# A hybrid attention and pooling layer in f32r parts: column sums and the bias look-up as two-part products, a norm's sums seven K steps later, one place for the indexer's query weights

## The chip, the core and the metric

One core of one Trainium2 chip runs the whole layer as one program. The metric is the device time of one execution in microseconds (us); a kernel's time is the median of its runs. A difference under 0.2% (2.0 us here) is about what a measurement of this kernel can't tell from no change.

## What is computed

A decoder layer on 272 tokens (16 meta tokens and 256 of the sequence) of width 2048, in float32:

```
p = h @ W_in        # q | latent c_kv (256) | indexer queries (16 x 64) | indexer key | head weights | pool channels
c_kv = rms_norm(c_kv, g)                      # sum of squares over the 256 latent channels
score = sum_h w[t,h] * relu(q_idx . k_idx);   keep the top 64 keys of each query
logits = q_abs . c_kv * s + rel_bias[t5_bucket(t - s)];   softmax;   values
mix = concat(attention, pooled windows) @ W_o
h = layer_norm(alpha*h + mix)                 # mean and variance over 2048 channels
f = conv_gated_ffn(h)                         # up product, width 3 conv, gelu gate, down product
out = layer_norm(alpha*h + f)
```

## The kernel before

Every product is made of parts in f32r: a value is split into an upper part (a copy in f32r, made on ACT, called hi or `[:, 0]`) and a remainder (value less upper part, made on DVE, lo or `[:, 1]`). A K step of a product is three matmuls: hi with hi, and the two mixed ones. `product` (lines 305 to 315) does this for 16 K steps in an order given by a list of places (`K_PROJ`, `K_O`, `K_UP`). A tile's flag `turned` sets which of the two mixed matmuls comes first.

A stream of weight blocks of 1 MB feeds it: SP issues the load of a raw block (3 buffers), ACT writes the upper parts (line 190) and DVE the remainders (line 191), in two halves of 1024 columns, into one of 3 split tiles. `weights()` hands out a block and starts the one two ahead. Where in a split tile the two parts start is given in bytes by `place`; `places` picks it for each block. The first 8 blocks are the indexer's queries and have eight places in `QUERIES`, of which the first is `(88, False)`.

The tokens are the partitions' free axis: activations lie as channels by tokens, so a sum over channels is a matmul with a matrix of ones (`sum_rows`, line 357). These matmuls, the one of the bias look-up (line 456) and the one of line 795 are in plain float32, and not in parts.

- Queries, lines 486 to 510: for each of 8 blocks j, the product in three pieces (9, 3 and 4 K steps) with the two heads of block j - 1 between them (`dots`, line 469: matmuls, two relus on ACT into a tile `rl`, two updates of `score` on DVE). After j = 0 comes `latent_scale` (line 427: the two squares `sqs` are summed, a DVE transposition into `r`, line 430 on DVE, and a power on POOL, line 431); after j = 1 come `latent_norm` and `relative_bias` (line 450: two small loads, the look-up as matmul of the table with a one-hot matrix, a strip to DRAM and back as `bias`).
- The tiles made by `temp` (`wt`, `sq`, `r`, `rb`, `rl`, `rb_sb`, `oh`, `strip` and later ones) share four buffers under one tag, "t", given out in the order of the program.
- Output and first norm, lines 740 to 800: 16 output blocks m; after m = 3 POOL adds four of them, after m = 4 their column sum gives an offset `acc` (lines 795 and 796). `about_k(m)` then takes the offset off (DVE, line 768), squares (ACT, 770), adds to the running sums `s1` and `s2` on POOL (774, 776) and makes a tile `fold` of the channel in two parts (ACT 781, DVE 782). The last channel, m = 15, is not added on POOL: its value and its square go as own matmuls into the sums.
- Up product, lines 968 to 1009: the first 8 up blocks (f < 4, two halves each) multiply `folded`, so that the norm's scale and shift can be put on behind the product (`unfold`). In the first of them, after 5 K steps, comes `deviation` (line 804): four float32 matmuls, two transpositions, some small DVE steps, a power on POOL (813), two row spreads (370). The second half of the third up block's remainder waits for it (`later`, line 223). Then `normalise` (825 to 830) makes the normed channels `h_parts`, some behind each block, for the up blocks from f = 4 on.

Each engine runs its queue in the order that a planner fixed when the program was built: it goes by the order of the program and by its own estimates of when an instruction can start, and an instruction whose inputs are late holds up those behind it on its engine.

Of the kernel before, what the change touches and what calls it, by code (L numbers as in the profile page):

```python
# [25 lines left out]
H = 8  # L26
# [87 lines left out]
def places(n, kind):  # L114
# [5 lines left out]
    if n < 8:  # L120
        return place(*QUERIES[n])
# [5 lines left out]
QUERIES = ((88, False), (96, True), (72, True), (152, True), (216, True), (40, False), (168, False), (232, True))  # L127
# [6 lines left out]
def tile_layer(ctx, tc, xt, w_first, w_proj, w_uk, w_uv, w_pool, w_o, w_up, w_down, cols, rows, rel_bias, onehot, out):  # L134
# [214 lines left out]
    ones = sb.tile([P, P], F32, name="ones")  # L349
    nc.vector.memset(ones, 1.0)  # L350
# [6 lines left out]
    def sum_rows(s):  # L357

        ps = small()
        for n, t in enumerate(s):  # L360
            nc.tensor.matmul(ps[:, :t.shape[1]], ones, t, start=n == 0, stop=n == len(s) - 1)
        return ps[:, :W]
# [48 lines left out]
    for j in range(2):  # L411
# [5 lines left out]
        sqs.append(sq)  # L417
    widx = ap_.tile([P, 2, HI], F32, name="widx")
# [8 lines left out]
    def latent_scale():  # L427
        r = temp([P, W], "r")
        to_partitions(r, sum_rows(sqs))
        nc.vector.tensor_scalar(v, r[:, ::32], 1.0 / C, EPS, op0=ALU.mult, op1=ALU.add)  # L430
        nc.gpsimd.tensor_tensor(v, v, half, op=ALU.pow)
# [18 lines left out]
    def relative_bias():  # L450
        rb_sb = temp([32, H], "rb_sb")
        nc.sync.dma_start(rb_sb, rel_bias)
        oh = temp([32, T], "oh")
        nc.sync.dma_start(oh, onehot)
        ps = small()
        nc.tensor.matmul(ps[:H, :T], rb_sb, oh, start=True, stop=True)
# [29 lines left out]
    for j in range(8):  # L486
# [17 lines left out]
        if j == 0:  # L504
            latent_scale()
        if j == 1:
            latent_norm()
            relative_bias()
# [250 lines left out]
    nc.gpsimd.memset(sums[:, 2 * NQ:], 0.0)  # L759
# [5 lines left out]
    def about_k(m):  # L765
# [7 lines left out]
        elif 1 < m < KT - 1:  # L773
            nc.gpsimd.tensor_tensor(s1, s1, yd, op=ALU.add)
        if 0 < m < KT - 1:
# [9 lines left out]
        return yd, sq  # L785

    for m in range(1, KT):
        output(m)
        if m == KC - 1:
            nc.gpsimd.tensor_tensor(acc, y[:, 0, Q0:], y[:, 1, Q0:], op=ALU.add)  # L790
            for k in range(2, KC):
                nc.gpsimd.tensor_tensor(acc, acc, y[:, k, Q0:], op=ALU.add)
        if m == KC:
            ps = small()
            nc.tensor.matmul(ps[:, :NQ], ones, acc, start=True, stop=True)
            nc.scalar.activation(acc, ps[:, :NQ], AF.Copy, scale=1.0 / (KC * P))
        if m >= KC:
            while len(folded) < min(m + 1, 2 * (m - KC + 1)):
                last_two = about_k(len(folded))

# [3 lines left out]
    def deviation():  # L804
        mean, square = (of_token[:, j * NQ:j * NQ + W] for j in range(2))
        for j, r in enumerate((mean, square)):
            to_partitions(r, sum_rows([sums[:, j * NQ:j * NQ + W], last_two[j]]))
# [135 lines left out]
    for item in plan:  # L943
# [48 lines left out]
        if f < FOLDED:  # L992
            k = 0
            if f + half_ == 0:
                product(ps[:, :NE], hl, folded, 0, NE, K_UP, k1=5)
                deviation()
                k = 5
# [110 lines left out]
    for i in range(2):  # L1108
# [25 lines left out]
        if i:  # L1134

            shift = small()
            nc.tensor.matmul(shift, ones[:1, :], gb[7][:1, :], start=True, stop=False)
# [71 lines left out]
```

## Time and profile before

| | |
|---|---|
| time, median of 3 runs | 1020.82 us (1019.65 to 1021.59) |
| the profiled execution: its time, its span | 1020.17 us, 1018.4 us |
| PE, matmul busy | 1010.6 us, 99% |
| DVE, ACT, POOL busy | 889.6 us (87%), 622.0 us (61%), 187.8 us (18%) |
| chain that ended last, by engine | PE 95%, issue 2%, DMA 1%, POOL 1% |
| HBM | 232.50 MB read, 230 GB/s over the span |

The span is the time from the first to the last instruction of the profiled execution; its time is 1.8 us longer. Starts in a timeline are us from the span's start. A matmul's duration in a row includes the pipeline behind it, so the cost of one is read from start to start: a K step (called a triple below) runs from one L312 row to the next.

### The profile page before, as it was taken

To read this page: it belongs to the slowest core of one execution; us is meant where nothing else is said; L and a number is where in the kernel's file an instruction comes from. 1 tells how busy PE (TensorE), PEld (TensorE's weight loads), DVE (VectorE), ACT (ScalarE), POOL (GpSimd) and SP (SyncE) were. 2 spreads that over 40 slices of the span, in tenths; PEclk is the share of its full clock that TensorE was granted. 3 is DMA by queue.
4 is the path that set the end of the run, shared out by engine and by line. 5 is a ranking of instruction groups with operands and counts; after the bars stand their busy time and mean duration, and the time that the engine had idled before them with its cause. 6 is when DMAs were issued, how large, how long until landed. Compare 5 with 4: busy or idle time off the path is not lost.

```text
span 1018.4 us, 19198 instructions
## 1 busy us (share of the span) xinstructions
PE 1010.6 (99%) x7644; PEld 963.1 (95%) x7644; DVE 889.6 (87%) x1401; ACT 622.0 (61%) x1000; POOL 187.8 (18%) x245
## 2 busy tenths in 40 slices
PE   9999999999999999999999999999999999999997
PEld 8999999999999999999999999999999999999986
DVE  6878668758879998999999998999999998999876
ACT  6656346655549765655666656666566666666675
POOL 1200014125430022111121111211112111120031
PEclk9999999999999999999999999999999999999998
DMA  8755643454654668989888798887988779888774
GB/s 327 253 190 213 226 159 108 135 203 166 207 177 155 207 192 256 291 288 291 288 295 279 275 301 271 284 288 274 302 278 288 275 283 287 279 288 283 285 223 160
DMA packets 59755, 250.28 MB, mean 246 GB/s; under 512 B 21735, under 2 KB 22417, under 8 KB 32657
## 3 DMA queue, kind: packets, MB, share of 16 engines
q1 hardware_dynamic: 34592, 230.42, 63.1%
q0 software_dynamic: 7888, 16.14, 8.3%
q10 hardware_dynamic: 17184, 2.49, 1.5%
q8 instruction: 60, 0.98, 0.4%
q14 instruction: 31, 0.25, 0.1%
HBM read 232.50 MB, written 2.11 MB: 230 GB/s over the span
## 4 chain that ended last, share of the span: by engine, by line
PE 95%; issue 2%; DMA 1%; POOL 1%; ACT 0%; DVE 0%; SPq 0%; POOLq 0%; ACTq 0%
PE mm L315 47%; PE mm L312 24%; PE at L909 6%; PE at L910 6%; PE at L911 6%; DMA wraw<-in_w_proj 1%; PE mm L962 1%; PE mm L961 1%; PE mm L963 1%; DMA wraw<-in_w_first 1%; POOL gb L1028 0%; PE mm L614 0%; PE at L649 0%; PE at L475 0%; PE at L476 0%
## 5 line engine op out<-in xcount | busy, mean ns | idle before, releaser
L191 DVE TENSOR_TENSOR whl<-wraw,whl 128x1024 fp32r<-128x1024 f32 (+1 forms) x415 | 484.8, 1204 | 40.0 <-ACT whl L190 39.3
L190 ACT ACTIVATE whl<-wraw 128x1024 fp32r<-128x1024 f32 (+1 forms) x415 | 401.4, 1014 | 117.6 <-DMA wraw<-in_w_up 26.0
L315 PE MATMUL mm<-hp,whl 128*128 128x258 f32 x2560 | 448.8, 279 | 0.0
L315 PEld LDWEIGHTS mm<-hp,whl 128*128 128x128 f32 x2560 | 389.7, 188 | 2.9
L312 PE MATMUL mm<-hp,whl 128*128 128x258 f32 x1280 | 356.5, 279 | 0.0
L312 PEld LDWEIGHTS mm<-hp,whl 128*128 128x128 f32 x1280 | 240.3, 188 | 2.8
L315 PE MATMUL mm<-xp,whl 128*128 128x256 f32 (+5 forms) x768 | 139.6, 282 | 0.3 <-DVE whl L191 0.3
L315 PEld LDWEIGHTS mm<-xp,whl 128*128 128x128 f32 x768 | 118.3, 188 | 0.9 <-DVE whl L191 0.5
L312 PE MATMUL mm<-xp,whl 128*128 128x256 f32 (+5 forms) x384 | 111.3, 290 | 0.0
L881 POOL TENSOR_TENSOR forms<-za 128x128 f32<-128x128 f32 x20 | 21.8, 1091 | 298.1 <-DVE za L862 231.9
L312 PEld LDWEIGHTS mm<-xp,whl 128*128 128x128 f32 x384 | 72.3, 188 | 1.0 <-issue 0.5
L910 PE MATMUL at<-whl,gp 128*128 128x512 f32 x180 | 70.5, 392 | 0.0
L911 PE MATMUL at<-whl,gp 128*128 128x512 f32 x180 | 70.4, 392 | 0.0
L844 ACT ACTIVATE z<-mm,cv 128x256 f32<-128x256 f32 x40 | 22.5, 563 | 77.8 <-PE mm L315 76.9
L909 PE MATMUL at<-whl,gp 128*128 128x512 f32 x180 | 69.1, 394 | 0.0
L844 ACT ACTIVATE za<-mm,cv 128x256 f32<-128x256 f32 x40 | 22.6, 564 | 65.6 <-PE mm L315 57.2
L884 POOL TENSOR_TENSOR forms<-za 128x128 f32<-128x128 f32 x20 | 20.4, 1018 | 196.7 <-DVE za L862 196.7
L315 PE MATMUL mm<-mixp,whl 128*128 128x258 f32 x256 | 45.4, 279 | 0.0
L315 PE MATMUL mm<-fold,whl 128*128 128x260 f32 x256 | 45.3, 279 | 0.0
L315 PE MATMUL mm<-mixa,whl 128*128 128x258 f32 x256 | 45.2, 278 | 0.0
L911 PEld LDWEIGHTS at<-whl,gp 128*128 128x128 f32 x180 | 33.8, 188 | 8.0
L910 PEld LDWEIGHTS at<-whl,gp 128*128 128x128 f32 x180 | 33.7, 187 | 6.4
(341 smaller groups left out, 1607.2 us busy)
## 6 DMA issues: line engine op xcount, KB each, us to landing
wraw<-in_w_up SPq DMA_DIRECT2D x88, 1024.0 KB, 5.1
wraw<-in_w_down SPq DMA_DIRECT2D x80, 1024.0 KB, 6.5
wraw<-in_w_proj SPq DMA_DIRECT2D x24, 1024.0 KB, 5.1
wraw<-in_w_o SPq DMA_DIRECT2D x16, 1024.0 KB, 4.9
y<-v POOLq DMA_DIRECT2D x27, 256.0 KB, 8.3
y<-u POOLq DMA_DIRECT2D x18, 256.0 KB, 4.8
wraw<-in_w_first SPq DMA_DIRECT2D x8, 304.0 KB, 5.5
x<-in_xt SPq DMA_DIRECT2D x1, 2176.0 KB, 8.2
```

The source lines that it names most:

```text
L190: upper = nc.scalar.activation(hl[:, 0, c], like(raw[:, c], hl, c), AF.Copy)
L191: lower = nc.vector.tensor_tensor(hl[:, 1, c], like(raw[:, c], hl, c), hl[:, 0, c].bitcast(F32), op=ALU.subtract)
L312: nc.tensor.matmul(ps, wh, ah, start=n == 0, stop=False)
L315: nc.tensor.matmul(ps, a, b, start=False, stop=i == 1 and n == KT - 1)
L844: nc.scalar.activation(z, src[:, 2:NQ], AF.Identity, bias=col(C_B, j), scale=col(C_W, 3 * j + 2))
L881: nc.gpsimd.tensor_tensor(s[:, 0], a21, a22, op=ALU.add)
L884: nc.gpsimd.tensor_tensor(s[:, 3], a11, a21, op=ALU.subtract)
L909: nc.tensor.matmul(ps, a[:, 0, i], hl[:, 0, w], start=j == 0, stop=False)
L910: nc.tensor.matmul(ps, a[:, 0, i], hl[:, 1, w], start=False, stop=False)
L911: nc.tensor.matmul(ps, a[:, 1, i], hl[:, 0, w], start=False, stop=j == n - 1)
L961: nc.tensor.matmul(downs[i], a[:, 0, r], hl[:, 0, w], start=k == 0, stop=False)
L962: nc.tensor.matmul(downs[i], a[:, 0, r], hl[:, 1, w], start=False, stop=False)
```

## The change

- The eight query blocks all lie at `place(88)`, not turned; `QUERIES` goes.
- `sum_rows` takes an upper part and a remainder, and makes two f32r matmuls with f32r ones instead of as many float32 ones as there were tiles.
- The two squares of the latent are added on POOL and split (ACT, POOL) before their sum. `latent_scale` and the look-up come after block j = 1, `latent_norm` after j = 2; the two small loads come after j = 0, and the one-hot matrix is loaded twice, into 64 partitions.
- The look-up multiplies the table's two parts, stacked in 64 partitions, by an f32r copy of the one-hot matrix (copied on POOL).
- The offset's sum is split (ACT, DVE) before its product.
- `about_k(15)` adds to `s1` and `s2` on POOL as the others do; both sums are then split (one ACT copy, one DVE subtraction of 2 x 258 columns), and `deviation` comes after 12 K steps of the first up block instead of 5.

```diff
@@ -118,13 +118,12 @@
     if n < 8:
-        return place(*QUERIES[n])
+        return place(88)
-QUERIES = ((88, False), (96, True), (72, True), (152, True), (216, True), (40, False), (168, False), (232, True))
@@ -346,20 +345,20 @@
-    ones = sb.tile([P, P], F32, name="ones")
-    nc.vector.memset(ones, 1.0)
+    ones = sb.tile([P, P], F32R, name="ones")
+    nc.vector.memset(ones.bitcast(F32), 1.0)
-    def sum_rows(s):
+    def sum_rows(hi, lo):
-        ps = small()
-        for n, t in enumerate(s):
-            nc.tensor.matmul(ps[:, :t.shape[1]], ones, t, start=n == 0, stop=n == len(s) - 1)
-        return ps[:, :W]
+        ps, one = small(), ones
+        nc.tensor.matmul(ps[:, :hi.shape[1]], one, hi, start=True, stop=False)
+        nc.tensor.matmul(ps[:, :lo.shape[1]], one, lo, start=False, stop=True)
+        return ps[:, :hi.shape[1]]
@@ -415,6 +414,10 @@
+    sq_parts = [ap_.tile([P, W], F32R, tag="t", name="sqp", bufs=4, padded_shape=[P, KW]) for _ in range(2)]
+    nc.gpsimd.tensor_tensor(sqs[0], sqs[0], sqs[1], op=ALU.add)
+    nc.scalar.activation(sq_parts[0], sqs[0], AF.Copy)
+    nc.gpsimd.tensor_tensor(sq_parts[1], sqs[0], sq_parts[0].bitcast(F32), op=ALU.subtract)
@@ -426,7 +429,7 @@
-        to_partitions(r, sum_rows(sqs))
+        to_partitions(r, sum_rows(*sq_parts))
@@ -447,13 +450,14 @@
-    def relative_bias():
-        rb_sb = temp([32, H], "rb_sb")
-        nc.sync.dma_start(rb_sb, rel_bias)
-        oh = temp([32, T], "oh")
-        nc.sync.dma_start(oh, onehot)
+    def relative_bias(rb_sb, oh_raw):
+        rb_parts = ap_.tile([64, H], F32R, tag="t", name="rb_parts", bufs=4, padded_shape=[P, KW])
+        nc.scalar.activation(rb_parts[:32], rb_sb, AF.Copy)
+        nc.vector.tensor_tensor(rb_parts[32:], rb_sb, rb_parts[:32].bitcast(F32), op=ALU.subtract)
+        oh = ap_.tile([64, T], F32R, tag="t", name="oh", bufs=4, padded_shape=[P, KW])
+        nc.gpsimd.tensor_copy(oh, oh_raw)
         ps = small()
-        nc.tensor.matmul(ps[:H, :T], rb_sb, oh, start=True, stop=True)
+        nc.tensor.matmul(ps[:H, :T], rb_parts, oh, start=True, stop=True)
@@ -502,10 +506,15 @@
         if j == 0:
+            rb_sb, oh_raw = temp([32, H], "rb_sb"), temp([64, T], "oh_raw")
+            nc.sync.dma_start(rb_sb, rel_bias)
+            for r in (0, 32):
+                nc.sync.dma_start(oh_raw[r:r + 32], onehot)
+        if j == 1:
             latent_scale()
-        if j == 1:
+            relative_bias(rb_sb, oh_raw)
+        if j == 2:
             latent_norm()
-            relative_bias()
@@ -756,7 +765,6 @@
-    nc.gpsimd.memset(sums[:, 2 * NQ:], 0.0)
@@ -770,9 +778,9 @@
-        elif 1 < m < KT - 1:
+        elif m > 1:
             nc.gpsimd.tensor_tensor(s1, s1, yd, op=ALU.add)
-        if 0 < m < KT - 1:
+        if m:
             nc.gpsimd.tensor_tensor(s2, s2, sq, op=ALU.add)
@@ -790,21 +800,28 @@
+            acc_parts = both_parts("accp")
+            acc_parts = [acc_parts[:, i, :NQ] for i in range(2)]
+            nc.scalar.activation(acc_parts[0], acc, AF.Copy)
+            nc.vector.tensor_tensor(acc_parts[1], acc, acc_parts[0].bitcast(F32), op=ALU.subtract)
         if m == KC:
-            ps = small()
-            nc.tensor.matmul(ps[:, :NQ], ones, acc, start=True, stop=True)
-            nc.scalar.activation(acc, ps[:, :NQ], AF.Copy, scale=1.0 / (KC * P))
+            ps = sum_rows(*acc_parts)
+            nc.scalar.activation(acc, ps, AF.Copy, scale=1.0 / (KC * P))
+    s_hi, s_lo = both_parts("s_hi"), both_parts("s_lo")
+    nc.gpsimd.memset(s_hi[:, :, NQ:].bitcast(F32), 0.0)
+    both_sums = sums[:, :2 * NQ].rearrange("p (a b) -> p a b", b=NQ)
+    nc.scalar.activation(s_hi[:, :, :NQ], both_sums, AF.Copy)
+    nc.vector.tensor_tensor(s_lo[:, :, :NQ], both_sums, s_hi[:, :, :NQ].bitcast(F32), op=ALU.subtract)
@@ deviation
-            to_partitions(r, sum_rows([sums[:, j * NQ:j * NQ + W], last_two[j]]))
+            to_partitions(r, sum_rows(s_hi[:, j], s_lo[:, j, :NQ]))
@@ -992,9 +1009,9 @@
-                product(ps[:, :NE], hl, folded, 0, NE, K_UP, k1=5)
+                product(ps[:, :NE], hl, folded, 0, NE, K_UP, k1=12)
                 deviation()
-                k = 5
+                k = 12
```

`both_parts` allots a tile of two parts from the ring of 24 activation slots that also holds `xp`, `mix` and `hp`.

## Rows read from the trace of the kernel before

**Rows 1.** The page's chain that ended last, shares of the span by engine

```profile
PE 95%; issue 2%; DMA 1%; POOL 1%; ACT 0%; DVE 0%; SPq 0%; POOLq 0%; ACTq 0%
```

**Rows 2.** Timeline of PE, block j = 0 (start, duration, engine, line, operation)

```profile
26.86 0.28 PE L312 MATMUL mm<-xp,whl 128*128 128x256 f32 x1
...
29.30 0.28 PE L312 MATMUL mm<-xp,whl 128*128 128x256 f32 x1
...
29.65 1.14 PE L361 MATMUL at<-sq,ones 128*128 128x288 f32 x4
...
30.98 0.28 PE L312 MATMUL mm<-xp,whl 128*128 128x256 f32 x1
```

**Rows 3.** Timeline of PE, block j = 6, its first nine K steps

```profile
64.73 0.28 PE L312 MATMUL mm<-xp,whl 128*128 128x256 f32 x1
...
67.97 0.28 PE L475 MATMUL at<-kidx,qi 128*128 128x256 f32 x1
```

**Rows 4.** Timeline of PE around the look-up

```profile
38.33 0.29 PE L312 MATMUL mm<-xp,whl 128*128 128x256 f32 x1
...
38.78 0.62 PE L456 MATMUL at<-oh,rb_sb 32*8 32x272 f32 x2
...
39.79 0.28 PE L312 MATMUL mm<-xp,whl 128*128 128x256 f32 x1
```

**Rows 5.** Timeline of PE around the offset's sum

```profile
235.64 0.28 PE L312 MATMUL mm<-mixp,whl 128*128 128x258 f32 x1
...
235.99 0.60 PE L795 MATMUL at<-acc,ones 128*128 128x258 f32 x2
...
236.78 0.28 PE L312 MATMUL mm<-mixp,whl 128*128 128x258 f32 x1
```

**Rows 6.** Timeline of PE around the norm's sums, and the eighth up block's start

```profile
298.86 0.28 PE L312 MATMUL mm<-fold,whl 128*128 128x260 f32 x1
...
301.42 0.28 PE L312 MATMUL mm<-fold,whl 128*128 128x260 f32 x1
...
338.87 0.28 PE L312 MATMUL mm<-fold,whl 128*128 128x260 f32 x1
```

**Rows 7.** Timeline of DVE: channel m = 14, then m = 15

```profile
292.10 0.42 DVE L751 SCALAR_TENSOR_TENSOR x<-x,mm 128x258 f32<-128x258 f32 x1 [0.86 <-PE mm L315]
...
293.24 1.61 DVE L191 TENSOR_TENSOR whl<-wraw,whl 128x1024 fp32r<-128x1024 f32 x1 [0.26 <-ACT whl L190]
294.77 0.86 DVE L782 SCALAR_TENSOR_TENSOR fold<-x,cv,fold 128x258 fp32r<-128x258 f32 x1
...
297.65 0.42 DVE L751 SCALAR_TENSOR_TENSOR x<-x,mm 128x258 f32<-128x258 f32 x1 [0.88 <-PE mm L315]
...
298.79 1.23 DVE L191 TENSOR_TENSOR whl<-wraw,whl 128x1024 fp32r<-128x1024 f32 x1 [0.26 <-ACT whl L190]
299.93 0.48 DVE L782 SCALAR_TENSOR_TENSOR fold<-x,cv,fold 128x258 fp32r<-128x258 f32 x1
```

**Rows 8.** Timeline of POOL: the sums of m = 14, then the powers and a copy

```profile
293.13 0.64 POOL L774 TENSOR_TENSOR sums<-sums,x 128x258 f32<-128x258 f32 x1 [3.32 <-DVE x L768]
293.73 1.62 POOL L776 TENSOR_TENSOR sums<-sums,sq 128x258 f32<-128x258 f32 x1
...
33.77 2.73 POOL L431 TENSOR_TENSOR rms_v<-rms_v,half 128x9 f32<-128x9 f32 x1 [29.84 <-DVE rms_v L430]
...
40.25 1.17 POOL L534 CAST few<-ctp 128x32 fp32r<-128x32 f32 x1 [0.76 <-DVE ctp L440]
```

**Rows 9.** Timeline of DVE: behind the norm's power; remainder of the eighth up block

```profile
305.01 0.17 DVE L814 SCALAR_TENSOR_TENSOR st<-st 128x9 f32<-128x9 f32 x1 [1.73 <-POOL st L813]
...
337.11 1.22 DVE L191 TENSOR_TENSOR whl<-wraw,whl 128x1024 fp32r<-128x1024 f32 x1
```

**Rows 10.** Stretches: us, PE, PEld, DVE, ACT, POOL busy (count), clock, DMA share, GB/s

```profile
305.00:325.00 20.00, 20.00 (x172) 20.00 (x172) 19.95 (x49) 17.45 (x31) 0.00 (x0) 1.00 0.43 155
325.00:345.00 20.00, 20.00 (x173) 20.00 (x172) 20.00 (x46) 17.48 (x32) 0.00 (x0) 1.00 0.47 158
```

More of the change, by code (lines that the diff above doesn't have):

```diff
@@ L784, in about_k, with both_parts @@
         folded.append(a)
-        return yd, sq
+    def both_parts(name):
+        return ring.tile([P, 2, WIDE], F32R, tag="act", name=name)
     for m in range(1, KT):
@@ L792, in tile_layer @@
                 nc.gpsimd.tensor_tensor(acc, acc, y[:, k, Q0:], op=ALU.add)
+            acc_parts = both_parts("accp")
+            acc_parts = [acc_parts[:, i, :NQ] for i in range(2)]
+            nc.scalar.activation(acc_parts[0], acc, AF.Copy)
+            nc.vector.tensor_tensor(acc_parts[1], acc, acc_parts[0].bitcast(F32), op=ALU.subtract)
         if m == KC:
-            ps = small()
-            nc.tensor.matmul(ps[:, :NQ], ones, acc, start=True, stop=True)
-            nc.scalar.activation(acc, ps[:, :NQ], AF.Copy, scale=1.0 / (KC * P))
+            ps = sum_rows(*acc_parts)
+            nc.scalar.activation(acc, ps, AF.Copy, scale=1.0 / (KC * P))
         if m >= KC:
             while len(folded) < min(m + 1, 2 * (m - KC + 1)):
-                last_two = about_k(len(folded))
+                about_k(len(folded))
+    s_hi, s_lo = both_parts("s_hi"), both_parts("s_lo")
[3 more added lines that the diff above has]
+    nc.vector.tensor_tensor(s_lo[:, :, :NQ], both_sums, s_hi[:, :, :NQ].bitcast(F32), op=ALU.subtract)
     st = fp.tile([P, 4, W // 32], F32, name="st", bufs=1)
@@ L1136, in tile_layer @@
             shift = small()
-            nc.tensor.matmul(shift, ones[:1, :], gb[7][:1, :], start=True, stop=False)
+            nc.tensor.matmul(shift, ones[:1, :].bitcast(F32), gb[7][:1, :], start=True, stop=False)
         deviation_of(i)
```

## The prediction, made before the change was run

> **What bounds the kernel now.** I read the chain that ended last before anything else: 95% of the span is PE, and no other engine has more than 1% [rows 1]. So what counts is PE's queue: what takes columns out of it is gained whole, and what makes it wait is lost whole. Other engines matter only where PE would wait for them. The next view is the timeline of PE, read from start to start, since a row's duration holds the pipeline: a triple (the three matmuls of a K step) of 256 columns takes (29.30 - 26.86) / 7 = 0.349 us in block j = 0 [rows 2], and (67.97 - 64.73) / 9 = 0.360 us in block j = 6 [rows 3]; one of 260 columns in the up product takes 0.353 us, as the 96 triples of the second to the seventh up block show, if 301.42 is taken as the first block's sixth triple: 10 more end it at 304.95, and (338.87 - 304.95) / 96 = 0.353 [rows 6]. Then the timelines of DVE and POOL around the first norm, for what each value of the sums waits for [rows 7, 8], and last the stretches behind it: DVE is busy 19.95 and 20.00 of 20 us there [rows 10]. So a DVE that falls behind at the norm stays behind for 40 us.
>
> **What the change takes off PE.** Four places, each by the distance of two L312 rows less the two triples between them.
> - The latent's squares: 30.98 - 29.30 = 1.68, less 2 x 0.349, is 0.98 for two float32 products of 288 columns [rows 2]. In f32r a 256-column product takes 0.349 / 3 = 0.116, so two of 288 take 2 x 0.116 x 288 / 256 = 0.26. Gain 0.72.
> - The look-up: 39.79 - 38.33 = 1.46, less 2 x 0.360, is 0.74 [rows 3, 4]. One product of 272 columns takes 0.12, whether 32 or 64 rows are filled (I take it so: no row here has 64). Gain 0.62.
> - The offset: 236.78 - 235.64 = 1.14, less two triples of 258 columns (0.353 x 258 / 260 = 0.350), is 0.44 [rows 5, 6]. Two products of 258 take 0.23. Gain 0.21. Its new split (an ACT copy, a DVE subtraction) has a whole output block of 5.6 us to lie beside; without that cover it would cost what the offset's consumers wait, and these are on DVE with a block of lead.
> - The norm's sums: 301.42 - 298.86 = 2.56, less 2 x 0.353, is 1.85 [rows 6]. Afterwards 2 x (288 + 258) columns take 0.49. Gain 1.36.
>
> Together 2.91. **The queries' place:** block 0 already lies at 88, not turned, and has the fastest triple of the two that I show. Were all seven others as slow as block 6, 88 would give 7 x 16 x (0.360 - 0.349) = 1.2; if block 0 is faster for another reason (nothing of `dots` runs in it), nothing. I take 0.65, the middle, since the other blocks' triples lie between the two. Gains: 3.56.
>
> **What it adds: three places where PE may wait.** The splits of the squares (two POOL operations, one ACT copy) have the whole of block 1 as cover. `latent_norm` a block later is needed only behind the eighth block. The small loads now stand one block earlier in SP's queue and wait there for a buffer of tag "t", with later weight loads behind them; a raw block's buffer comes free only when an older block is split, so I cost that at nothing; if that cover were gone, a query block's remainder would be late, and PE with it.
>
> **(a) The last channel's tile.** K_UP has channel 15 in the eighth place. The first up block starts at 298.86 - 4 x 0.353 = 297.45 [rows 6]. Without the sums in front, its eighth triple asks for the remainder of `fold` 15 (third matmul of a turned block) at 297.45 + 7 x 0.353 + 0.235 = 300.16. Now that tile was ready at 299.93 + 0.48 = 300.41, and the sums, at the sixth place, hid it [rows 7]. And it comes later now, because channel 15 gets the POOL additions that channel 14 has: with these beside it, DVE took 1.61 for the weights' remainder and 0.86 for the tile, against 1.23 and 0.48 for channel 15 [rows 7, 8]. From the start of line 751 to the tile's end it is 295.63 - 292.10 = 3.53 for channel 14, so 297.65 + 3.53 = 301.18 for channel 15. PE waits 1.02: I take 1.0. The low end is 300.41 - 300.16 = 0.25. The Trainium skill (SBUF — State Buffer, "Who interferes with whom") says that a DVE and a GpSimd instruction which share the port pair do not slow each other but that the second fully blocks until the first is done. The rows show less: POOL's first addition ran 293.13 to 293.77 and the DVE instruction of 293.24 lost 0.4 and not 0.5, and the pair behind overlapped for the most part. By the page's rule the four would run one after another (293.77, 294.98, 295.63, 296.11), the tile would come 0.48 later, and the sum below would be 0.48 higher.
>
> The sums themselves then stand behind four more triples, at 301.3 + 4 x 0.353 = 302.7. POOL's last addition ends at 298.7 + 0.64 + 1.62 = 301.0, and an ACT copy and a DVE subtraction of 516 columns (each under the 1.2 of a 1024-column remainder [rows 7]; I take 0.6 and 0.7) end at 302.3. No wait there, with 0.4 to spare.
>
> **(b) The look-up.** Count the four buffers of "t" after block 0: two parts of the squares, the table, the raw one-hot matrix. The relus of `dots` in block 1 get one only when the sums' product has run, at the block's end; then `r` gets the first relu's, the table's parts the second's, and the f32r one-hot matrix gets that of `r`, when line 430 is done. Line 430 also starts the power, which comes first in the program and so, I expect, in POOL's queue: 2.73 us [rows 8], and only then the copy. PE has the look-up in its queue and waits there with all of block 2 behind it. How much depends on how long the planner took the power to be. Where something stood behind a power before, it waited 1.73 [rows 9]. Bounds: 0, if the copy goes first or PE's queue has the look-up late enough; 3.7, if the whole power and the difference of a copy under contention (1.17 for 32 columns [rows 8]) are unplanned. I take the row that it is nearest to: 1.7.
>
> **(c) A late remainder behind the norm.** The norm's sums move on PE from 299.21 to 302.7, 3.5 later; the first pair is 0.92 - 0.25 = 0.67 shorter, so DVE's chain behind them (transpositions, power, row spreads, `normalise`) starts 2.8 later. DVE has no idle time in the 40 us behind [rows 10]. The eighth up block starts at 338.87 and asks for its first remainder with its second matmul, at 338.99; it was ready at 337.11 + 1.22 = 338.33 [rows 6, 9]. That is 0.66 to spare, and PE comes 0.36 earlier (1.36 gained, 1.0 lost). So PE waits 2.8 + 0.36 - 0.66 = 2.5 there, if DVE does the same work in the same order. The one place to make it up is the wait for the power, 1.73 [rows 9]: the next block's remainders are ready there only from about 305.5 on (its split tile is freed as the first up block ends, and then ACT works 1.0), and the power now ends at 305.0 + 2.8 = 307.8, so one half of 1.22 fits in [rows 9]. Bounds 0 and 2.5; I take 2.5 - 1.2 = 1.3.
>
> **The sum.** -3.56 + 1.0 + 1.7 + 1.3 = +0.4 us, against 1020.17 of the profiled execution: 1020.6. The median of the three runs is 0.65 above that execution, so as a median 1021.2.
>
> **The rivals.**
> - *The covers hold.* The planner puts the copy ahead of the power, or the look-up late in PE's queue, and DVE fills its wait with both halves, or takes the blocks' remainders before the last `normalise`: (b) and (c) near nothing. Then -3.56 + 1.0 = -2.6, 1018.2 as a median. For it: the chain shows a PE that hardly waits anywhere [rows 1], so the planner's orders do fit this chip mostly. Against it: the 1.73 behind a power [rows 9], and a DVE without slack [rows 10].
> - *The look-up stands behind the whole power.* POOL runs the power, then a slowed copy, and (b) is 3.7: -3.56 + 1.0 + 3.7 + 1.3 = +2.4, 1023.3 as a median. It ends over the bound of 0.2% as soon as (b) is over 3.3, or at (b) = 2.1 if (c) is at its full 2.5. For it: the count of buffers, which leaves the copy no earlier place. Against it: the planner may know the power's length.
> - *The change doesn't do what it says:* the place 88 gives nothing with `dots` beside it, or f32r products with ones cost more than the rows of other products. That takes up to 0.65 + 0.5 from the gains: 1022.3.
>
> **How the numbers follow.** My sum 0.39, the covers 0.28, the look-up 0.26, the last 0.07. The likeliest is the sum: 1021.2, with its own range 1019.5 to 1022.8. The range for 8 in 10 takes in the covers (1018.2, and a little under for 1.2 from the place) and the look-up (1023.3, with (c) at its bound 1024.5): 1017.8 to 1024.3. About 0.2%, 2.0 us, is what a measurement of this kernel can tell from no change. Faster by more than that: 0.28; within: 0.42; slower by more: 0.30.
>
> **What would show it.** In the timeline of PE: a wait of about 1 us in the first up block before the third matmul of channel 15, ended by DVE line 782; a wait in front of the look-up's product in block 2, ended by POOL's copy, with the power just before it on POOL; a wait at the start of the seventh or eighth up block, ended by DVE line 191. The sums' products should take 0.26, 0.12, 0.23 and 0.49 us, and the triples of blocks 1 to 7 0.349. The prediction is wrong if PE's waits sum to under 2 us or over 6, or if the triples of the queries don't come down.

## The result, and the profile after

The changed kernel takes 1029.60 us (median of 5 runs, 1028.27 to 1032.01) against 1020.82 us: a ratio of 1.0091 (95% interval 1.0079 to 1.0102), 9 us slower. The forecast was 1021.2, in a range of 1017.8 to 1024.3. The profiled execution of the changed kernel is its longest: 1032.01 us, span 1030.2 us, 11.8 more than before's.

The view of waits of PE (line that waited, releaser; us in total, times, longest) has three new rows against before, and they are the three of the prediction: (b) 2.3 us, (c) 1.5 and (a) 0.9. The view of after:

```profile
PE at L460 <- POOL oh L458: 2.3, 1, 2.3
PE mm L314 <- DVE whl L190: 1.5, 1, 1.5
PE at L1116 <- ACT diag L1114: 1.5, 1, 1.5
PE mm L314 <- DVE fold L790: 0.9, 1, 0.9
PE at L156 <- PEq L1215: 0.8, 1, 0.8
PE mm L1133 <- DVE whl L302: 0.3, 1, 0.3
PE mm L385 <- ACT whl L337: 0.2, 1, 0.2
```

and of before:

```profile
PE at L1099 <- ACT diag L1097: 1.5, 1, 1.5
PE at L157 <- PEq L1198: 0.8, 1, 0.8
PE mm L315 <- DVE whl L191: 0.3, 1, 0.3
PE mm L1116 <- DVE whl L303: 0.2, 1, 0.2
PE mm L386 <- ACT whl L338: 0.2, 1, 0.2
```

The three new rows are 4.7 us of waits, against 3.4 of gains (below). So this view leaves some 10 of the 11.8 us unexplained. Most of them are in products that wait for nothing. The groups of PE by line and shape in the stretch 252 to 290 us, where both kernels run output blocks (count | busy us, mean ns of one | idle before), show before's 331 products of 258 columns in 38 us, each 278 ns long:

```profile
L315 PE MATMUL mm<-mixp,whl 128*128 128x258 f32 x112 | 19.7, 278 | 0.0
L315 PE MATMUL mm<-mixa,whl 128*128 128x258 f32 x109 | 19.3, 278 | 0.0
L312 PE MATMUL mm<-mixp,whl 128*128 128x258 f32 x56 | 15.6, 278 | 0.0
L312 PE MATMUL mm<-mixa,whl 128*128 128x258 f32 x54 | 15.0, 278 | 0.0
```

and after's 313 in the same time, 283 ns long, and 289 the first of a triple, with no idle time before any of them:

```profile
L314 PE MATMUL mm<-mixa,whl 128*128 128x258 f32 x108 | 20.1, 283 | 0.0
L314 PE MATMUL mm<-mixp,whl 128*128 128x258 f32 x101 | 18.8, 283 | 0.0
L311 PE MATMUL mm<-mixa,whl 128*128 128x258 f32 x54 | 15.6, 289 | 0.0
L311 PE MATMUL mm<-mixp,whl 128*128 128x258 f32 x50 | 14.4, 289 | 0.0
```

From start to start (PE's timeline, the first product of the second block behind the offset's sum and of the last output block, nine blocks of 48 products apart): in the changed kernel

```profile
244.58 0.29 PE L311 MATMUL mm<-mixp,whl 128*128 128x258 f32 x1
...
297.38 0.29 PE L311 MATMUL mm<-mixp,whl 128*128 128x258 f32 x1
```

52.80 / 432 = 122.2 ns a product, and in the kernel before

```profile
241.98 0.28 PE L312 MATMUL mm<-mixp,whl 128*128 128x258 f32 x1
...
291.90 0.28 PE L312 MATMUL mm<-mixp,whl 128*128 128x258 f32 x1
```

49.92 / 432 = 115.6 ns. The granted clock is 1.00 in all of this, and by the two programs' allocations the products of the output blocks read the same addresses and write the same PSUM banks. The expectations below call it the gait; here it is the **pace**. It changes at one point: the block in front of the offset's sum still runs at 115.6 ns, and all 11 behind it at 122. Nine up blocks (the first that multiply the normed channels, 353 to 405 us) are at 122.3 as well, 115.6 before; the stretch 361 to 388 us shows their products 283 ns long:

```profile
L314 PE MATMUL mm<-hp,whl 128*128 128x258 f32 x150 | 27.5, 283 | 0.0
```

Together: 11 x 48 x 6.7 ns = 3.5 us and 9 x 48 x 6.7 ns = 2.9 us, and 0.2 for the two up blocks of 260 columns ahead of these (120.0 for 117.8).

One more loss stands behind the wait for the look-up. By stretches (us, PE, PEld, DVE, ACT, POOL busy, clock, DMA share, GB/s):

```profile
44.00:45.00 1.00, 1.00 (x7) 1.00 (x7) 0.29 (x2) 0.50 (x2) 0.00 (x0) 0.50 0.64 254
45.00:46.00 1.00, 1.00 (x6) 1.00 (x6) 0.82 (x3) 0.58 (x2) 0.28 (x1) 0.50 1.06 451
46.00:47.00 1.00, 1.00 (x7) 1.00 (x6) 0.58 (x2) 0.29 (x1) 0.49 (x1) 0.50 0.55 229
48.00:80.00 32.00, 32.00 (x274) 32.00 (x274) 25.06 (x44) 20.42 (x42) 4.00 (x5) 1.00 0.59 187
```

The granted clock fell to 0.50 (1.2 of 2.4 GHz) after PE had stood for 2.3 us, and products start 0.21 to 0.23 us apart (the first 0.32) from 43.56 to 46.92: 15 products in 3.36 us that take 1.8 at 2.4 GHz, so 1.6 us are lost.

The account of the two profiled executions, from row to row:

| | forecast | measured |
|---|---|---|
| squares' sums | -0.72 | -0.71 |
| look-up's product | -0.62 | -0.43 |
| offset's sum | -0.21 | -0.21 |
| norm's sums | -1.36 | -1.35 |
| queries at 88 | -0.65 | -0.66 |
| wait (a), channel 15's tile | +1.0 | +1.1 |
| wait (b), the look-up | +1.7 | +2.3 |
| wait (c), seventh and eighth up block | +1.3 | +2.2 |
| clock behind (b) | - | +1.6 |
| pace: 11 output blocks, 2 + 9 up blocks | - | +6.6 |
| sum | +0.4 | +10.4 |

The waits are taken from start to start, less a product's usual distance, and with the slower product behind each wait, so (a) and (c) are over the view's. Of the 1.4 left of the 11.8, 1.3 lie where the change does nothing: 0.4 ahead of the first query block (its first product starts at 23.47 us, 23.08 before; 23.2 to 25.0 in the other traces), 0.9 behind the start of the last block of products (61.0 to 62.8 us from there to the end in all traces).

The gains' rows: squares 36.43 - 36.16 = 0.27, and the norm's four products 309.26 - 308.76 = 0.50 [rows 2, 6]:

```profile
36.16 0.30 PE L359 MATMUL at<-sqp,ones 128*128 128x288 f32 x1
36.30 0.29 PE L360 MATMUL at<-sqp,ones 128*128 128x288 f32 x1
36.43 0.28 PE L311 MATMUL mm<-xp,whl 128*128 128x256 f32 x1
...
308.76 0.29 PE L359 MATMUL at<-s_hi,ones 128*128 128x288 f32 x1
...
309.26 0.29 PE L311 MATMUL mm<-fold,whl 128*128 128x260 f32 x1
```

Query block j = 6 now has a triple of (70.63 - 67.51) / 9 = 0.347 us, 0.360 before [rows 3]:

```profile
67.51 0.28 PE L311 MATMUL mm<-xp,whl 128*128 128x256 f32 x1
...
70.63 0.28 PE L479 MATMUL at<-kidx,qi 128*128 128x256 f32 x1
```

### The profile page after: what moved, and what is told of

It is laid out like the page before. It is cut to its first block, busy times and chain, and to the rows that moved or that the text cites. A ratio compares the mean times of both kernels' runs of the same rounds, so it can differ in the third digit from the quotient of the medians.

```text
span 1030.2 us, 19193 instructions
## 1 busy us (share of the span) xinstructions
PE 1017.7 (99%) x7637; PEld 970.0 (94%) x7637; DVE 891.6 (87%) x1404; ACT 624.5 (61%) x1004; POOL 194.1 (19%) x250
## 4 chain that ended last, share of the span: by engine, by line
PE 89%; DVE 4%; issue 3%; DMA 1%; POOL 1%; ACT 1%; SPq 0%; POOLq 0%; DVEq 0%; ACTq 0%
PE mm L314 44%; PE mm L311 22%; PE at L926 6%; PE at L927 6%; PE at L928 6%; PE mm L385 2%; DVE whl L190 2%; DMA wraw<-in_w_down 1%; DVE x L842 0%; DVE hp L847 0%; PE at L479 0%; DVE x L843 0%; ACT whl L189 0%; POOL gb L1045 0%; DMA wraw<-in_w_first 0%
## 5 line engine op out<-in xcount | busy, mean ns | idle before, releaser
L190 DVE TENSOR_TENSOR whl<-wraw,whl 128x1024 fp32r<-128x1024 f32 (+1 forms) x415 | 485.4, 1204 | 41.9 <-ACT whl L189 40.8
L898 POOL TENSOR_TENSOR forms<-za 128x128 f32<-128x128 f32 x20 | 23.0, 1148 | 292.0 <-DVE za L879 228.4
L901 POOL TENSOR_TENSOR forms<-za 128x128 f32<-128x128 f32 x20 | 21.7, 1083 | 202.8 <-DVE za L879 188.8
L314 PEld LDWEIGHTS mm<-fold,whl 128*128 128x128 f32 x256 | 39.3, 188 | 3.1 <-DVE whl L190 2.1
L928 PEld LDWEIGHTS at<-whl,gp 128*128 128x128 f32 x180 | 33.8, 188 | 8.0
## 6 DMA issues: line engine op xcount, KB each, us to landing
wraw<-in_w_up SPq DMA_DIRECT2D x88, 1024.0 KB, 5.0
wraw<-in_w_down SPq DMA_DIRECT2D x80, 1024.0 KB, 6.7
wraw<-in_w_proj SPq DMA_DIRECT2D x24, 1024.0 KB, 5.1
wraw<-in_w_o SPq DMA_DIRECT2D x16, 1024.0 KB, 4.9
```

The costliest lines, as they stand in the source:

```text
L190: lower = nc.vector.tensor_tensor(hl[:, 1, c], like(raw[:, c], hl, c), hl[:, 0, c].bitcast(F32), op=ALU.subtract)
L314: nc.tensor.matmul(ps, a, b, start=False, stop=i == 1 and n == KT - 1)
L898: nc.gpsimd.tensor_tensor(s[:, 0], a21, a22, op=ALU.add)
L901: nc.gpsimd.tensor_tensor(s[:, 3], a11, a21, op=ALU.subtract)
L928: nc.tensor.matmul(ps, a[:, 1, i], hl[:, 0, w], start=False, stop=j == n - 1)
```

## The experiments

Two questions: are the three waits and their prices as predicted, and what sets the pace. The labels that begin with b are the kernel before with one piece of the change; those with a are the changed kernel with one piece undone or mended. "Pace" is the mean distance from start to start within a block, in ns, of the profiled execution; ratios are to the kernel before, timed beside the run.

| run | median us | ratio (95%) | pace, output blocks behind the offset | pace, up blocks behind the eighth |
|---|---|---|---|---|
| before | 1020.8 | | 115.6 | 115.6 |
| after | 1029.6 | 1.0091 (1.0079 to 1.0102) | 122.3 | 122.3 |
| b_offset | 1023.8 | 1.0037 (1.0025 to 1.0049) | 122.3 | 115.6 |
| b_alike | 1022.9 | 1.0019 (1.0009 to 1.0030) | 122.3 | 115.6 |
| b_three | 1022.0 | 1.0013 (1.0003 to 1.0024) | 117.8 | 115.6 |
| b_f32end | 1024.2 | 1.0045 (1.0032 to 1.0058) | 122.3 | 115.6 |
| b_late | 1024.0 | 1.0036 (1.0024 to 1.0047) | 115.6 | 115.6 |
| a_led | 1027.4 | 1.0071 (1.0057 to 1.0086) | 115.6 | 122.3 |
| a_uled | 1024.9 | 1.0043 (1.0029 to 1.0056) | 115.6 | 115.6 |
| a_norm | 1025.1 | 1.0060 (1.0044 to 1.0077) | 122.3 | 115.6 |
| a_onehot | 1025.2 | 1.0058 (1.0045 to 1.0071) | 122.3 | 122.3 |
| a_fold15 | 1030.3 | 1.0091 (1.0074 to 1.0107) | 122.3 | 115.6 |
| a_again | 1030.1 | 1.0094 (1.0075 to 1.0112) | 122.3 | 122.3 |
| a_best | 1019.4 | 0.9992 (0.9983 to 1.0001) | 115.6 | 115.6 |
| a_best2 | 1017.9 | 0.9980 (0.9971 to 0.9988) | 115.6 | 115.6 |

**b_offset: the offset's sum alone.**

```diff
+            acc_parts = ring.tile([P, 2, WIDE], F32R, tag="act", name="accp")
...
-            nc.tensor.matmul(ps[:, :NQ], ones, acc, start=True, stop=True)
+            for i in range(2):
+                nc.tensor.matmul(ps[:, :NQ], ones_r, acc_parts[i], start=i == 0, stop=i == 1)
```

> The kernel before with one part of the change: the offset's sum as two f32r products of a split tile. Theory G (gait): TensorE has two steady gaits for the same products at the same addresses, 115.6 ns and 122.3 ns from start to start for 258 columns; the two short products between two output blocks put it into the slow one, where it stays until another shape of product comes. Then the 11 output blocks behind the offset take 48 x 6.7 ns = 0.32 us more each, 3.5 in all, less the 0.2 that the sum itself saves: +3.3 us, about 1024.1, and the weight load starts 2 ns behind its product's start there instead of 4. Rival T (traffic): the slow products of the changed kernel come from what DVE, ACT and POOL do beside them later on (sums, split); then this part alone gives -0.2 us, about 1020.6, and the rate stays 115.6.

Measured 1023.84, 4.1 over the kernel before in the same runs; from the offset to the end of the output blocks the trace gives 3.3 of it. The same stretch 252 to 290 us shows the long products, with none of the rest of the change in the program:

```profile
L315 PE MATMUL mm<-mixa,whl 128*128 128x258 f32 x110 | 20.4, 283 | 0.0
L312 PE MATMUL mm<-mixa,whl 128*128 128x258 f32 x54 | 15.6, 289 | 0.0
```

Theory G holds: two f32r products, worth 0.2 us, cost 3.5 in the blocks behind them. Traffic on other engines is out, since this kernel has before's. By the records in ns, the weight load starts 2 ns (median) behind its product's start in these blocks, and 4 ns in the kernel before.

**a_led: another place for the first four K steps of two blocks.**

```diff
-    return led(224) if n in (10, 11, 27, 28) else place(96, True)
+    return led(224) if n in (10, 11, 27, 28, 31, 32) else place(96, True)
```

> The changed kernel, and the two weight blocks behind the offset laid out as the blocks 27 and 28 of the stream are (first four K steps at another place). Theory G: those four K steps put TensorE back into the fast gait, as in the blocks 27 and 28, and output blocks from the second or third on run at 115.6 ns: 9 to 11 blocks x 0.32 = 2.9 to 3.5 us less than the changed kernel, 1026.4. The waits of the first up block and of the seventh and eighth stay (0.9, 0.4, 1.8 us). Rival T: place has nothing to do with it, the rate stays at 122.3 and the time at 1029.6.

Block 31 of the stream stays at 121.8, block 32 runs at 116.5, and from the next one on all are at 115.6:

```profile
L314 PE MATMUL mm<-mixa,whl 128*128 128x258 f32 x112 | 19.7, 278 | 0.0
```

3.1 us less from the offset to the end of the output blocks in the trace, and 0.0020 off the ratio, whose interval still overlaps that of after. So the pace is kept from block to block until something changes it, and a few products at another place can change it back. The program alone doesn't fix it: the second output block (block 27 of the stream) runs at 121.3 here and at 116.7 in a_uled, which is the same program up to block 50.

**b_alike, b_three, b_f32end: what about the two products does it.** b_alike puts the ones and the two parts at the bytes that a weight block and an activation have:

```diff
+            acc_parts = Parts(ring.tile([P, 2, WIDE], F32R, tag="act", name="accp"), 18, NQ).parts
+            ones_a = ring.tile([P, 2, WIDE], F32R, tag="act", name="ones_a")[:, 0, 16:16 + P]
...
```

> The kernel before with the offset's sum as two f32r products, as in the run of that part alone, but with its ones and its two parts laid out in their tiles like a weight block and an activation of the output product (ones at byte 96 of 256, upper part at 104, remainder at 176). Theory G1: what throws TensorE into the slow gait is that the two inserted products read other places than the block's own; then nothing is disturbed here, the 11 blocks run at 115.6 ns, and the part gives its 0.2 us: 1020.3, with the kernel before at 1020.5. Rival G2: the count of two alone (a triple is three) or the other product width of load decides: 122.3 ns again and +3.3, 1023.8.

b_three adds a third f32r product with zeros; b_f32end adds a float32 product of 32 columns of zeros instead:

```diff
...
+            for i in range(3):
+                nc.tensor.matmul(ps[:, :NQ], ones_r, (acc_parts + [zero])[i], start=i == 0, stop=i == 2)
```

> The kernel before with the offset's sum in f32r, as in the run of that part alone, and a third product of the ones with a tile of zeros behind the two (it adds nothing to the sum). Theory N: the number of products put in between decides; a triple is three, so with three the gait comes out of the sum as it went in, and the 11 output blocks run at 115.6 ns: 0.1 us over the kernel before for the third product less 0.2 of the sum, about 1020.4. Rival H: it is the hand-over from products of another weight tile in f32r as such, whatever their number: 122.3 ns, and 3.4 us over, 1023.9.

> The same, with a float32 product of 32 columns of zeros as the third in place of an f32r one. Theory H': the kernel before keeps the fast gait because its sum is a float32 product, behind which the next product starts late (236.23 to 236.54 us there, 0.31 us instead of 0.12); any float32 product as the last of the sum does the same, and the 11 blocks run at 115.6 ns: about 1020.5. Rival: the gait is lost at the entry into the f32r products, and what stands last does not bring it back: 122.3 ns and 3.4 us over, 1023.9.

Place alone (G1) falls: 122.3 in b_alike. So does H': a float32 product at the end leaves 122.3. b_three shows a **third** pace, neither the fast nor the slow one, kept for all 11 blocks:

```profile
L315 PE MATMUL mm<-mixp,whl 128*128 128x258 f32 x112 | 20.1, 280 | 0.0
```

So a third f32r product changes the pace that follows (against H), but three do not leave it as it was (against N). Whether the third counts by its number or by what it reads isn't told apart, and what picks one of the three paces stays open.

**a_onehot: the copy ahead of the power.**

```diff
+            oh_parts = ap_.tile([64, T], F32R, name="oh")
+            nc.gpsimd.tensor_copy(oh_parts, oh_raw)
         if j == 1:
             latent_scale()
...
```

> The changed kernel, but the one-hot matrix is copied into a tile of its own, right behind its load and so ahead of the power on POOL. Theory W: the wait of 2.26 us in front of the look-up is the power, and the stretch behind it at a granted clock of 0.50 (43.6 to 46.9 us, products 0.21 us apart instead of 0.12) follows from that wait and from nothing else. Then both go: 2.3 + 1.7 = 4.0 us less, 1025.6, and the granted clock stays 1.00. Rival S: the look-up then waits for its table's remainder on DVE or for something else in the same stretch, and the wait is only renamed: 0 to 1 us less, about 1029.

Measured 1025.22, 4.4 under the changed kernel (0.0033 by the ratios). In the trace, which is of its longest execution (1029.30, the others 1024.6 to 1025.7), the look-up's wait is 0.8, for DVE's half of the table, not 2.3 for POOL, and the clock stays at 1.00. Rival S is right about the 0.8 and W about the wait's cause; that the half clock needs this wait fits the record (it stands in the query blocks of none of the nine traces without it), though it doesn't follow each time (see a_again).

**a_norm: the norm's sums as before.** Undoes the last bullet of the change.

> The changed kernel with the norm's sums as before (channel 15 not added on POOL, float32 products after 5 K steps). Theory D: the waits of the first up block (0.9) and of the seventh and eighth (0.4 and 1.8) go, and with the last of these the entry into the slow gait, so that the nine up blocks behind them run at 115.6 instead of 122.3 ns (2.9 us) and the eighth at 117.8 instead of 120.1 (0.2); 1.36 us of products come back: -0.9 - 2.2 - 3.1 + 1.4 = -4.8 us, 1024.8. Rival P: the nine blocks are slow because their activation tiles lie in other slots of the ring, which the offset's tile still shifts by one here; then they stay at 122.3 and the gain is 1.9, 1027.7.

Measured 1025.12. The rows of `whl` L190 and `fold` are gone from the waits, and the nine up blocks run at 115.6, though the offset's tile still shifts some of their slots. Rival P falls with a_fold15 below: there the first two of the nine read their activations at the very addresses of after, and run at 115.6.

**b_late: only the place of the norm's sums.**

```diff
-                product(ps[:, :NE], hl, folded, 0, NE, K_UP, k1=5)
+                product(ps[:, :NE], hl, folded, 0, NE, K_UP, k1=12)
...
```

> The kernel before with one part of the change: the norm's sums (still float32, channel 15 still apart) after 12 K steps of the first up block instead of 5. Theory D: the place alone makes DVE's chain late by 7 x 0.353 = 2.5 us; 0.66 us are to spare at the eighth up block, so TensorE waits there for a remainder of DVE, 1 to 1.9 us, and 0.25 for channel 15's tile; that wait breaks the fast gait, and the nine blocks behind it run at 122.3 ns: 2.9 us more. In all 4.1 to 5.1 us over the kernel before, about 1024.3. Rival F: it is the f32r sums that break the gait and not the wait; then 1.2 to 2.2 us over, about 1021.5, with 115.6 ns in those nine blocks.

Measured 1023.98. The wait is there without any f32r sum, and larger than I had it: 0.5 at the seventh and 2.3 at the eighth up block from start to start, 2.9 in all:

```profile
PE mm L315 <- DVE whl L191: 2.3, 2, 2.1
```

But the up blocks behind it run at 115.6. So a wait doesn't always bring the slow pace. F's 115.6 came, but F isn't shown either: a_fold15 has the f32r sums and 115.6 too. No wait is listed for channel 15's tile, because one of the sums' products runs just ahead of the product that reads it (L312 at 301.08 is the first of that triple):

```profile
301.32 0.65 PE L361 MATMUL at<-sums,ones 128*128 128x288 f32 x2
301.63 0.45 PE L315 MATMUL mm<-fold,whl 128*128 128x260 f32 x1
...
301.10 0.48 DVE L782 SCALAR_TENSOR_TENSOR fold<-x,cv,fold 128x258 fp32r<-128x258 f32 x1
```

The tile is ready at 301.58, 0.26 behind 301.32, where its product would have been due: the low end of (a), 0.25, fits.

**a_uled: both stretches laid out again.** As a_led, and `led(224)` for the first two up blocks that read the normed channels.

> The changed kernel with four blocks laid out as the blocks 27 and 28 are (first four K steps at another place): the two behind the offset, and the first two of the up blocks that read the normed channels. Theory G: both slow stretches go but for a block or two (11 output blocks and 9 up blocks at 115.6 instead of 122.3 ns), while the three waits stay: 3.1 + 2.6 = 5.7 us less than the changed kernel, about 1024. Rival P: the up blocks keep their 122.3 ns whatever the place, since their tiles lie in other slots: 3.1 less, 1026.5.

Measured 1024.86, and both paces are fast, with the three waits as before (2.3, 1.6, 0.9). For the output blocks the rows are those of a_led. For the up blocks the run doesn't show that the place undid a slow pace of the wait: the eighth block already runs at 117.9 behind its wait, as in the two traces that stay fast anyway (see a_again). The first of the two blocks with the new place then falls into 122 by its ninth K step, and the four K steps of the second bring 115.6. Against after that is 4.7 us, where the rows from the offset to the end of the output blocks and from the seventh up block on give 5.8.

**a_fold15: channel 15 last.**

```diff
-K_UP = (1, 3, 5, 7, 8, 10, 12, 15, 0, 2, 4, 6, 9, 11, 13, 14)
+K_UP = (1, 3, 5, 7, 8, 10, 12, 14, 0, 2, 4, 6, 9, 11, 13, 15)
```

> The changed kernel with channel 15 as the last instead of the eighth K step of the up product. Theory B (given back): the wait of 0.90 us for channel 15's tile goes, but the sums, ready at 308.1 us by the trace, are then asked for at 303.25 + 12 x 0.354 = 307.5, so 0.6 us of it come back there; the other 0.3 come back at the seventh and eighth up block, since DVE's chain starts no earlier: no difference from the changed kernel, 1029.6, with waits of 0.6 (s_lo) and 2.5 (whl) instead of 0.9 and 2.2. Rival A: the tile's wait is a cost of its own, and 0.9 us are gained: 1028.7.

Measured 1030.29, the ratio of after. The trace is of one of its shorter executions (1028.20, from 1027.69 to 1032.37), and its nine up blocks run at the fast pace, which after's don't:

```profile
L314 PE MATMUL mm<-hp,whl 128*128 128x258 f32 x157 | 27.3, 278 | 0.0
```

So the median can't tell B from A, and the rows have to. The wait for the tile is gone, one of 0.3 for `s_lo` stands at the sums, and from the start of the seventh up block to the end of the eighth PE waits 2.5 instead of 2.2: of the 0.5 gained, 0.3 are given back. Mostly theory B, with 0.2 that stay and are too small for the times to show.

**a_again: the changed kernel once more.**

> The changed kernel itself once more. Theory R: three things of its profile are not the program's: the half clock behind the wait for the look-up (1.7 us), the slow gait of the nine up blocks behind the wait at the eighth (2.9), and they come in some executions and not in others, while the slow gait of the 11 output blocks and the three waits (2.3, 0.9, 2.2) are there in each. Then this execution shows the 11 blocks at 122.3 and the waits, and need not show the other two; its time is 1032 less 1.7 and 2.9 for each that is absent. Rival: all belong to the program, and the same rows come again at 1031 to 1032.

1031.41 in the profiled execution and 1028.68 in the other. All rows came again, the half clock (0.50 from 44 to 47 us) and the slow up blocks among them, so theory R is not shown. But over all traces the two are not bound to their waits. Of six with a wait of 2.2 to 2.3 us for the look-up, four show the half clock (after, a_again, a_uled, a_fold15), and two don't; a_led has the same wait and then

```profile
46.00:47.00 1.00, 1.00 (x10) 1.00 (x10) 0.73 (x3) 1.00 (x4) 0.00 (x0) 1.00 0.89 360
```

Of six with a wait of 1.8 to 2.3 at the eighth up block and no new layout behind it, four go on at 122.3 (after, a_again, a_led, a_onehot) and two at 115.6 (b_late, a_fold15). In the four, the eighth block itself runs at 120.0 behind its wait, in the two at 117.9: the pace is taken up at the end of the wait. The two are also the longest waits of the six (2.2 and 2.3 from start to start, against 1.8 to 1.9); a_uled's 1.9 with 117.9 behind it speaks against the length alone, and what decides stays open.

**a_best, a_best2: what is worth keeping.** The squares, the look-up and the queries' place; the offset in float32 as before; the norm's sums after 5 K steps, 15 channels of them in f32r parts and channel 15 in float32.

> What the runs leave of the change: the squares' f32r sum, the look-up with both of its split operands made early in tiles of their own, and the place of the queries; the offset in float32 as before (one product then hands over to the fast gait); the norm's sums after 5 K steps with channel 15 apart in float32 and the sums of the other 15 channels split while the last output block runs. Theory G with D and W: no wait of the three, no slow gait, gains 0.72 + 0.62 + 0.65 + 0.47 = 2.5 us less some 0.4 of waits on DVE's query remainders in the second query block: 2.1 us under the kernel before, 1018.2. Rival: any change ahead of the output blocks shifts the gait anew, and a stretch of them runs at 122.3: 1 to 4 us over, 1021 to 1024.

Measured 1019.36: no slow pace in the two stretches, no (a), (b) or (c). The rival has a small part: the second output block runs at 121.8 (116.6 before), 0.25 us, and the next is fast again; a_best2 has the same. The profiled execution, the longest of 11 (1021.01), has a wait of another kind in the second query block, for a relu on ACT:

```profile
35.88 0.39 PE L474 MATMUL at<-kidx,qi 128*128 128x256 f32 x1 [1.39 <-ACT rl L477]
```

ACT stood before it for a weight block. The load that it waits for was issued ahead of the small loads, at 24.83:

```profile
24.83 0.33 SPq L195 DMA_DIRECT2D wraw<-in_w_proj  x1
28.21 0.34 SPq L505 DMA_DIRECT2D rb_sb<-in_rel_bias  x1
29.96 0.82 SPq L507 DMA_DIRECT2D oh_raw<-in_onehot  x2
...
32.86 1.06 ACT L189 ACTIVATE whl<-wraw 128x1024 fp32r<-128x1024 f32 x1 [2.03 <-DMA wraw<-in_w_proj]
```

By the trace it landed 8.0 us after its issue. This load, the fourth of the query weights, takes 4.8 to 5.1 us in ten of the fifteen traces, after's among them, and 7.4 to 8.0 in four (b_late, a_norm, a_again, a_best), of which b_late issues its small loads later. So a slow landing in this execution is what the trace shows, and not the small loads.

a_best2 gives both loads to POOL's queue and tiles of their own, and the copy of the table to POOL.

> The version with the parts that gain, its two small loads moved from SP's queue to POOL's and into tiles of their own, and the table's upper part copied on POOL too. Theory Q: the wait of 1.4 us for a relu in the second query block is a weight block's load, issued 3 us late because the small loads stand before it in SP's queue and wait for a buffer (ACT waits 2.03 us for it with the relu behind). Then the wait goes, and the time is 1.4 us lower than that version's 1019.4: 1018.0. Rival: the weight load was late on its own account and ACT still waits: 1019.4.

Measured 1017.91, 0.9980 (0.9971 to 0.9988): 2.0 us under the kernel before by the ratio, and no wait over 0.3 us is left but those of before. The wait for the relu is gone in this trace, but the same load lands in 4.9 us here, so theory Q isn't shown; by the rows of a_best its rival is right, that the load was late on its own account. Why the median is 1.4 us under a_best's stays open; the intervals of the two ratios overlap.

## Why the prediction was wrong

**The step that failed** is one that the working took without saying so: that a triple costs the same before and behind an inserted product, so that each edit's price is "the distance of two L312 rows less the two triples between them". Four of the five gains came out that way to 0.01 (table above). But the offset's edit, costed at -0.21, changed the pace of the 11 blocks behind it, +3.5; b_offset and a_led show this. Behind the wait (c), which cost its own 2.2, the pace cost another 3.1. There a_norm shows no more than that without the wait the pace is fast: with such a wait it is slow in four traces of six. Of the 10.0 us between the two sums of the table the pace is 6.6, the half clock 1.6, (c) 0.9, (b) 0.6, and all the rest 0.3. The rows could have hinted at it: triples of one width cost 0.349 and 0.360 in two query blocks [rows 2, 3], so width alone doesn't set a product's cost; for the queries it was places, as the measured -0.66 bears out. I had no rival that says "an inserted product can change the speed of those that follow", and the range ended 5 us short. The signs named for being wrong didn't come: PE's new waits sum to 4.7 us in the view and 5.6 in the table, between 2 and 6, and the queries' triples came down. None of them looked at products that wait for nothing. Two slips in the working change no result: 301.42 starts the seventh triple and not the sixth (ten more do end at 304.95), and the last rival adds up to 1022.4.

**(a)** held: 1.02 predicted, 0.90 in the view of waits. The four operations behind it ran as forecast, from DVE's

```profile
304.58 1.62 DVE L190 TENSOR_TENSOR whl<-wraw,whl 128x1024 fp32r<-128x1024 f32 x1 [0.26 <-ACT whl L189]
306.13 0.86 DVE L790 SCALAR_TENSOR_TENSOR fold<-x,cv,fold 128x258 fp32r<-128x258 f32 x1
```

the tile is ready 306.99 - 303.44 = 3.55 us behind the start of the addition of the last block, 3.53 predicted (that addition, L760 here, starts at 303.44). The Trainium skill's full blocking (SBUF — State Buffer, "Who interferes with whom") would have put it 0.48 later by the prediction's estimate; this trace doesn't agree with the rule, as before's did not. The 0.90 is no price of its own, though: a_fold15 takes it away, and most of what that frees comes back.

**(b)** had the right mechanism and the wrong size, 2.3 for 1.7: the buffer chain is as counted, and the copy follows the power on POOL,

```profile
41.09 1.82 POOL L434 TENSOR_TENSOR rms_v<-rms_v,half 128x9 f32<-128x9 f32 x1 [11.15 <-PE mm L314]
42.89 0.40 POOL L458 CAST oh<-oh_raw 64x272 fp32r<-64x272 f32 x1
43.34 0.28 PE L460 MATMUL at<-oh,rb_parts 64*8 64x272 f32 x1 [2.26 <-POOL oh L458]
```

with a power of 1.82 and not of 2.73 [rows 8]. What wasn't in it is the half clock behind the wait, 1.6 more, which the working put at nothing without a word.

**(c)** was in its bounds (0 to 2.5) at 2.2; the value taken, 1.3, supposed that DVE would do half a remainder while it waits for the power. It did a remainder (L222) there, as before, and stood idle for 1.73 again. b_late, with 2.9, shows that the place alone is enough.

**The gains** were right but for the look-up, which the working took to cost 0.12 whether 32 or 64 rows are filled. In a_best2, where nothing waits around it, it takes 0.31 from start to start and not 0.12: the product of 64 rows starts 0.22 behind the one ahead of it, and the next 0.22 behind it.

```profile
36.66 0.29 PE L360 MATMUL at<-sqp,ones 128*128 128x288 f32 x1
36.88 0.29 PE L455 MATMUL at<-oh,rb_parts 64*8 64x272 f32 x1
37.10 0.39 PE L311 MATMUL mm<-xp,whl 128*128 128x256 f32 x1
```

**The small loads**, costed at nothing with the cover named, have no price that a trace shows. **The rivals:** "behind the whole power" had the mechanism of (b), at 2.3 where it said 3.7, and was still 6 us short; "the covers hold" and "doesn't do what it says" are out.

## What to carry to other kernels

On an engine that is busy 99% of the time, a product put between two blocks can have two prices: its own time, and the pace that it leaves behind. Compare the mean duration of one (278, 280 or 283 and 289 ns here) in the blocks ahead of it and behind it, and give a change of pace its own term, blocks x products x difference, in the range. A wait that a change adds can have the same second price; and a wait that you remove is a gain only if the one behind it isn't late too.

## What the runs showed of the hardware

- The same f32r products of 258 columns, at the same addresses and a granted clock of 1.00, ran at one of three steady paces: 115.6, 117.8 or 122.3 ns from start to start. They kept it over 500 products; in these runs two or three f32r products in between, the end of a wait, or four K steps read from another place came with a change of it. The Trainium skill (TensorE: Matmul & The Clock Gate, "Back-to-back issue gap") gives an isolated product at full clock a distance that follows from its width alone, and a stream one distance each at 128 and 512 columns; these rows have three for one width.
- After PE had stood for 2.2 to 2.3 us, the granted clock fell to 0.50 in four traces of six; behind the waits (c), up to 2.3 us from start to start, it stayed at 1.00.
- The one product of 64 rows by 8 between products of 128 by 128 cost 0.2 us more than its columns (0.31 for 0.12 in a_best2).
- A weight load of 1 MB (the fourth of the query weights) landed in 4.8 to 5.1 us in ten traces and in 7.4 to 8.0 in four.
